# Two stream encoder layer: the first 256 tokens transposed on TensorE during the modulation, modulation weights loaded by rows, modulation columns applied as scalars

## The chip, the core and the metric

One core of a Trainium2 chip. The metric is device time in microseconds, the median of several executions. One further execution was taken with the hardware profiler; all rows below are from it.

## What is computed

One layer for a prompt of 2048 tokens and a sample of 64 tokens with a cache of 128, model width 1024. The reference, cut to what matters here:

```python
mod = jax.nn.silu(c) @ w_ada + b_ada                 # (1024) @ (1024, 3072)
shift, scale, gate = jnp.split(mod, 3, axis=-1)
h = rms_norm(x, norm_g) * (1.0 + scale[:, None, :]) + shift[:, None, :]
u = h @ w_in                                         # columns: qa, ka, va, za, qb, kb, vb, fb, zb
...
oa_blk = diff_attention(...)                         # 4 heads, two score maps each
ob_blk = forgetting_attention(...)                   # 8 heads, score bias from cumulated log forget values
...
o = jnp.concatenate([ga, gb], axis=-1) @ w_out       # ga, gb: outputs times silu(z)
return x + gate[:, None, :] * o
```

So nothing of the projection can start before shift and scale are known, and they need the first 2048 columns of w_ada (8 MB).

## The kernel before, in words

**Order of the work.** Every instruction is first recorded in a plan, with a position; the class Plan then gives each a due time from estimated durations, a latency table and the table SHIFT (one offset per kind of operation and stage), and writes for each engine (PE, ACT, DVE, POOL and the DMA queue SP) one fixed order. Engines work in their order and wait for each other by semaphores. So a change of one cost or offset moves instructions everywhere.

**Numbers.** Matrices are split into two fp16 parts, hi and lo, under scales that are powers of two; a product is three fp16 matmuls. The scale of h comes from a bound on its peak (`sig_h`), that of a weight group from its peak (`w_max`, `w_peak`, `w_sigma`), after which `w_split` makes hi on ACT and lo on DVE, slice by slice, in a ring of 17 buffers.

**Main part.** w_in is worked through in eight groups of 512 columns (order 0, 1, 4, 5, 6, 7, 2, 3); group 0 and 1 run interleaved. For each of 8 token blocks of 256: project (q, 24 matmuls of 512 columns per 128 tokens and group), evacuate to u, normalize, rotate (POOL), transpose u on PE (tr), scores S, exponentials (E), probabilities split and transposed by DMA (PB to PT), values (po), output og. The transposed h of all blocks (hT) is kept in DRAM for the later groups. At the end og is projected by w_out (y).

**The start, which the change touches.** SP issues in order: conditioning vectors, constants, group 0's eight weight slices (wc), then 8 modulation tiles (wada) with the first 256 tokens x_0 and x_1 between, then group 1's slices. Each wada tile holds two k-slices of one half of the columns (`load_ada`: 512 shift and 512 scale columns, so rows of 2 KB). `mod_mm` multiplies them by silu(c) of prompt and sample (2 weight columns) into two column groups of 32 PSUM partitions; first all eight k of half 0, then of half 1. After each half: `mod_evac` (ACT shift rows, DVE (1 + scale) * norm_g), `mod_max` (peaks), `mod_rows` (PE spreads the prompt's row over 128 partitions), `mod_store` (rows to DRAM, from where `mod_load` later spreads them over partitions for the other blocks). For the first 256 tokens `h_first` applies the rows with tokens on partitions (4 passes a half), then `h_first_split` makes hi and lo and `h_first_trans` transposes them by DMA into hT, which the first projection matmuls q of group 0 read.

Matmuls into po that have ident_b on both sides (`warm`) compute nothing; they only keep PE busy before and between these steps. Group 1's peak is spread over the partitions through DRAM (`spread`, `gather`: tiles wmx_d and wrow), group 0's by a transpose and a matmul (`all_max_mm`).

Of the kernel before, what the change touches and what calls it, by code (L numbers as in the profile page):

```python
# [41 lines left out]
class Plan:  # L42
# [24 lines left out]
        'ep_square ACT': (1222, 7059, 69075, 100316, 33946, 17761, -559, 7791, -55499),
        'ep_square DVE': (-19737, -11205, -6053, -6235, 13891, -12021, 5467, -9194, -18777),
        'ep_square SP d': (17731, 2644, -20421, 44685, -453, 17057, 7365, -5250, -5933),
        'ep_trans PE': (-8510, 1413, 20757, 14554, 4162, -22993, -38513, -7700, 0),  # L70
        'ep_v ACT': (77357, 78843, 94474, 106969, 15393, 26795, 14839, 59051, 0),
        'ep_v DVE': (123205, 212871, 14149, 83229, 170299, 16014, -443, 779, 0),
        'f_evac ACT': (0, 283107, 0, 0, 0, 0, 0, 0, 0),
        'f_evac DVE': (0, 28121, 0, 0, 0, 0, 0, 0, 0),
        'first h0 ACT': (-47637, 0, 0, 0, 0, 0, 0, 0, 0),
        'first h0 DVE': (39992, 0, 0, 0, 0, 0, 0, 0, 0),
        'first h0 SP d': (-43600, 0, 0, 0, 0, 0, 0, 0, 0),
        'first h1 ACT': (20737, 0, 0, 0, 0, 0, 0, 0, 0),
        'first h1 DVE': (-3029, 0, 0, 0, 0, 0, 0, 0, 0),
        'first h1 SP d': (-3083, 0, 0, 0, 0, 0, 0, 0, 0),  # L80
        'first w ACT': (-1750, 0, 0, 0, 0, 0, 0, 0, 0),
        'first w DVE': (2329, 0, 0, 0, 0, 0, 0, 0, 0),
        'first w PE': (-14065, 0, 0, 0, 0, 0, 0, 0, 0),
        'first w POOL': (14606, 0, 0, 0, 0, 0, 0, 0, 0),
        'first x ACT': (-27378, 0, 0, 0, 0, 0, 0, 0, 0),
        'first x POOL': (148021, 0, 0, 0, 0, 0, 0, 0, 0),
# [9 lines left out]
        'gate_out ACT': (0, 0, 2849, 0, 0, 0, 0, 0, 0),  # L96
        'gate_out SP d': (0, 0, 77357, 0, 0, 0, 0, 0, 0),
        'gate_scale DVE': (0, 0, 0, 0, 0, 0, 0, 942, 38016),
        'h_load SP d': (-15270, 27231, 30875, 38614, 21795, -15328, 60179, -34016, 0),
# [455 lines left out]
def hybrid_layer_kernel(ctx: ExitStack, tc: tile.TileContext, x_prompt, x_sample, cache_a_k, cache_a_v,  # L555
# [1371 lines left out]
```

## Time and profile before

| | |
|---|---|
| median of 3 runs | 1626.23 us (1624.32 to 1629.85) |
| the profiled execution, its own time | 1624.04 us |
| its span (first to last instruction) | 1622.3 us |
| busy: PE, DVE, ACT, POOL | 1441.1, 1261.6, 928.9, 495.6 us |
| mean granted clock of TensorE | 0.966 of full |
| DMA | 298.5 MB, mean 184 GB/s |
| first projection matmul | at 70.3 us of the span |

In the rows an instruction is named by engine, operation and its tiles (out<-in). Every operation is issued from one helper, so all have the line L551, and tiles tell them apart. A wait in brackets is the idle time of that engine before the row, with what ended it. PE is the matmul part of TensorE, SPq the DMA queue's issues. The clock of 1.00 is 2.4 GHz, 0.50 is 1.2 GHz.

### The profile page before, as it was taken

To read this page: it belongs to the slowest core of one execution; us is meant where nothing else is said; L and a number is where in the kernel's file an instruction comes from. 1 tells how busy PE (TensorE), PEld (TensorE's weight loads), DVE (VectorE), ACT (ScalarE), POOL (GpSimd) and SP (SyncE) were. 2 spreads that over 40 slices of the span, in tenths; PEclk is the share of its full clock that TensorE was granted. 3 is DMA by queue.
4 is the path that set the end of the run, shared out by engine and by line. 5 is a ranking of instruction groups with operands and counts; after the bars stand their busy time and mean duration, and the time that the engine had idled before them with its cause. 6 is when DMAs were issued, how large, how long until landed. Compare 5 with 4: busy or idle time off the path is not lost. (4 is left out here: it accounts for less than half of the span.)

```text
span 1622.3 us, 29643 instructions
## 1 busy us (share of the span) xinstructions
PE 1441.1 (89%) x10900; PEld 729.1 (45%) x10900; DVE 1261.6 (78%) x2619; ACT 928.9 (57%) x1768; POOL 495.6 (31%) x620
## 2 busy tenths in 40 slices
PE   7499987888999988998889889988999899698998
PEld 3144444443454444444444444444444454344443
DVE  4588999978969886988678867986899789797431
ACT  2257765655567665775667656865665566453100
POOL 0056663324322121111212112112355354412322
PEclk9699999989999999999999999999999999899999
DMA  9758789957978899999999999999858664889772
GB/s 314 127 156 195 198 186 233 157 110 178 208 152 175 199 201 208 199 212 209 217 164 210 196 197 215 206 192 203 204 151 153 132 156 124 159 168 231 199 196 70
DMA packets 630414, 298.50 MB, mean 184 GB/s; under 512 B 513183, under 2 KB 601007, under 8 KB 623484
## 3 DMA queue, kind: packets, MB, share of 16 engines
q1 hardware_dynamic: 630268, 296.61, 85.1%
q8 instruction: 85, 1.39, 0.4%
q14 instruction: 61, 0.49, 0.1%
HBM read 129.12 MB, written 43.16 MB: 106 GB/s over the span
## 5 line engine op out<-in xcount | busy, mean ns | idle before, releaser
L551 PE MATMUL q<-wc,hT 128*128 128x512 f16 x3072 | 733.4, 383 | 27.3 <-DMA hT<-hl 17.3
L551 PEld LDWEIGHTS <-hT 128*128 128x128 f16 x3328 | 293.8, 98 | 336.6 <-issue 31.8
L551 ACT ACTIVATE E<-E,st 128x128 f32<-128x128 f32 (+15 forms) x256 | 305.9, 1196 | 158.7 <-DVE st L551 80.6
L551 PE MATMUL po<-VT,PT 128*128 128x128 f16 x3808 | 247.7, 215 | 82.3 <-DMA PT<-PB 44.6
L551 PEld LDWEIGHTS <-PT 128*128 128x128 f16 x3808 | 213.3, 100 | 154.1 <-DMA PT<-PB 69.2
L551 PE MATMUL S<-KT,qT 64*128 64x512 f16 (+3 forms) x1920 | 227.2, 355 | 17.8 <-DVE E L551 14.8
L551 DVE SCALAR_TENSOR_TENSOR PB<-E,PB 128x128 f16<-128x128 f32 (+15 forms) x128 | 164.2, 1298 | 33.7 <-ACT PB L551 32.9
L551 PE MATMUL y<-wc,ogT 128*128 128x512 f16 (+1 forms) x800 | 177.1, 380 | 2.5 <-DVE os_e L551 1.3
L551 POOL TENSOR_SCALAR rs<-rs 128x8 f32<-128x8 f32 (+1 forms) x72 | 20.6, 285 | 518.4 <-DVE rs L551 491.9
L551 ACT ACTIVATE PB<-E 128x128 f16<-128x128 f32 (+15 forms) x128 | 138.3, 1102 | 46.3 <-DMA PT<-PB 45.7
L551 DVE CUSTOM_DVE_ANT_0 E<-S,nk,cf 128x1024 f32<-128x1024 f32 (+7 forms) x128 | 131.5, 1045 | 42.6 <-PE S L551 42.4
L551 PEld LDWEIGHTS <-qT 64*128 64x128 f16 x1920 | 83.9, 95 | 143.6 <-issue 77.4
L551 DVE TENSOR_SCALAR_CACHE_REDUCE E<-S,cf 128x1024 f32<-128x1024 f32 (+7 forms) x128 | 131.4, 1042 | 13.0 <-PE S L551 12.7
L551 POOL TENSOR_TENSOR u<-u,gain 128x512 f32<-128x512 f32 (+1 forms) x72 | 96.1, 1335 | 98.1 <-DVE u L551 23.7
L551 POOL TENSOR_TENSOR rs<-rs,mhalf 128x8 f32<-128x8 f32 (+1 forms) x72 | 118.3, 1643 | 6.0
L551 PEld LDWEIGHTS <-ogT 128*128 128x128 f16 (+1 forms) x800 | 75.8, 98 | 95.9 <-issue 10.9
L551 ACT ACTIVATE u<-q,us 128x384 f32<-128x384 f32 x128 | 73.1, 572 | 75.4 <-PE q L551 37.3
L551 ACT ACTIVATE PB<-E,st 128x128 f16<-128x128 f32 (+7 forms) x64 | 76.6, 1198 | 41.1 <-DVE E L551 14.3
L551 DVE SCALAR_TENSOR_TENSOR PB<-E,st,PB 128x128 f16<-128x128 f32 (+8 forms) x64 | 87.6, 1369 | 9.7 <-ACT PB L551 9.4
L551 POOL TENSOR_TENSOR yt<-yt,xr 128x512 f32<-128x512 f32 (+1 forms) x34 | 44.0, 1295 | 142.4 <-DVE yt L551 116.0
L551 POOL TENSOR_SCALAR oar<-oar 128x1 f32<-128x1 f32 (+1 forms) x68 | 38.2, 562 | 155.6 <-ACT og L551 152.7
L551 ACT ACTIVATE og<-po,us 128x128 f32<-128x128 f32 x128 | 45.9, 359 | 60.9 <-PE po L551 51.5
(210 smaller groups left out, 1778.8 us busy)
## 6 DMA issues: line engine op xcount, KB each, us to landing
hT<-hTd SPq DMA_DIRECT2D x53, 1024.0 KB
out_dram<-u SPq DMA_DIRECT2D x128, 128.0 KB
wc<-in_w_in_dram SPq DMA_DIRECT2D x32, 256.0 KB
wada<-in_w_ada_dram SPq DMA_DIRECT2D x16, 512.0 KB
x<-in_x_prompt_dram SPq DMA_DIRECT2D x16, 512.0 KB
hTd<-hT SPq DMA_DIRECT2D x16, 512.0 KB
ogd<-og SPq DMA_DIRECT2D x64, 128.0 KB
nk<-nck_d SPq DMA_DIRECT2D x16, 512.0 KB
```

Of the source, the lines that this page charges most:

```text
L551: fn(*a, **kw)
```

## The change

- wada tiles hold one k-slice of all 2048 columns (rows of 8 KB, for the last three tiles two rows of 4 KB). `mod_mm(k)` multiplies all four column groups (half and shift or scale) per k.
- One DVE pass evacuates all four groups (adding 0 or 1 by `mod1`, multiplying by 1 or norm_g in `grow`), one takes the peaks. PE transposes the rows, so that shift and scale stand as columns with the model dimension on partitions (`mcol`, already times `sig_h`).
- The first 256 tokens are multiplied by their root mean square on ACT (in `h_first_x`) and transposed by PE into PSUM while the modulation runs (x_0 after k = 4, x_1 after k = 6). `h_first(k)` then applies scale and shift as two per-partition scalars and makes hi and lo straight in hT: 8 x (DVE, ACT, DVE) on 128x256. The four DMA transposes are gone.
- The rows go to DRAM only after that. Group 1's peak goes through PE too.
- Fewer warming matmuls: 88 instead of 102.
- The planner's costs of a matmul with few weight columns and of early DMA are changed, and the whole table SHIFT.

```diff
     SHIFT = {
...
-        'mod DVE': (-41547, 0, 0, 0, 0, 0, 0, 0, 0),
...
-        'w_sigma DVE': (-87292, 37584, 108307, 13840, 127334, -17687, -9035, 0, 0),
...
+        'w_sigma DVE': (-62083, 179110, 2508, 16863, 28799, -16180, 137089, 0, 0),
+        'w_sigma PE': (-27708, 0, 0, 0, 0, 0, 0, 0, 0),
...
-            return max(25.0, n / 2.4 * (0.55 if self.count(ar[0]) <= 32 else 1) + 2.5)
+            return max(25.0, n / 2.4 * (0.16 if self.count(ar[0]) <= 32 else 1) + 2.5)
...
-            return (560.0 if eng == "SP" else 400.0), tot * size / 300.0 * max(1.0, 512.0 / max(row, 64))
+            return (560.0 if eng == "SP" else 400.0), tot * size / (390.0 if self.pos < -90 else 300.0) * max(1.0, 512.0 / max(row, 64))
...
+    def load_ada(k):
+
+        tag, bufs = ADA_TAGS[k]
         if tag == "PT":
-            t = [st([128, 2, 512], F32, f"wada{n}_{i}", tag=tag, bufs=bufs) for i in range(2)]
+            t = [st([128, D], F32, f"wada{k}_{i}", tag=tag, bufs=bufs) for i in range(2)]
+            for i in range(2):
+                sp.dma_start(out=t[i], in_=wada_v[:, k, i * D:i * D + D])
         else:
-            t = st([128, 2, 2, 512], F32, f"wada{n}", tag=tag, bufs=bufs)
+            t = st([128, 2, D], F32, f"wada{k}", tag=tag, bufs=bufs)
+            sp.dma_start(out=t.rearrange("p s c -> p (s c)"), in_=wada_v[:, k, 0:2 * D])
             t = [t[:, i] for i in range(2)]
...
+    dve.memset(grow, 1.0)
...
-        if g:
+        if g > 1:
             spread(g, m)
...
-        if g == 0:
-            all_max_mm(mod_ps["S0"][:, 512:1024], m[:, 0:1], m[:, 1:2])
+        if g < 2:
+            all_max_mm(O_tile() if g else mod_ps["S0"][:, 512:1024], m[:, 0:1], m[:, 1:2])
...
-    WARM0, WARM1 = 9, 10
+    WARM0, WARM1 = 4, 3
...
+    def mod_mm(k):
+        for hf in range(2):
+            for s in range(2):
+                c, o = 32 * (2 * hf + s), s * D + hf * 512
+                if k == 0:
+                    pe.matmul(mod_ps["p"][c:c + 2, :], ones[0:1, 0:2], bada[0:1, o:o + 512], start=True, stop=False)
+        for hf in range(2):
+            for s in range(2):
+                c = 32 * (2 * hf + s)
+                pe.matmul(mod_ps["p"][c:c + 2, :], cs[:, k, :], ada_w[k][s][:, hf * 512:hf * 512 + 512], start=False, stop=(k == KC - 1))
+
+    def mod_evac():
+
+        dve.scalar_tensor_tensor(out=modr, in0=mod_ps["p"], scalar=mod1, in1=grow, op0=ALU.add, op1=ALU.mult)
+        dve.tensor_reduce(out=hb[:, 0:1], in_=modr, axis=AX, op=ALU.max, apply_absolute_value=True)
+
+    def mod_cols():
+
+        c = mod_ps["c"] = Q_tile("modc")
+        for q in range(4):
+            pe.transpose(c[:, q * 128:q * 128 + 128], modr[:, q * 128:q * 128 + 128], ident)
...
+    def h_first_x(t):
+
+        x = x_t[0, t]
+        act.activation(out=x, in_=x, func=AF.Copy, scale=hrs[0, t][:, 1:2])
+        for k in range(KC):
+            c = k % 4 * 256 + t * 128
+            pe.transpose(mod_ps[f"S{k // 4}"][:, c:c + 128], x[:, k * 128:k * 128 + 128], ident)
+
+    def h_first(k):
+
+        if k == 0:
             hT[0, 0] = st([128, 16, 256], F16, "hT0_0", tag="hT", bufs=2)
...
+        p = mod_ps[f"S{k // 4}"][:, k % 4 * 256:k % 4 * 256 + 256]
+        x = x_t[0, k // 4][:, k % 4 * 256:k % 4 * 256 + 256]
+        hi, lo = hT[0, 0][:, 2 * k, :], hT[0, 0][:, 2 * k + 1, :]
+        dve.tensor_scalar(out=x, in0=p, scalar1=mcol[:, 1, k:k + 1], scalar2=mcol[:, 0, k:k + 1], op0=ALU.mult, op1=ALU.add)
+        act.activation(out=hi, in_=x, func=AF.Copy)
+        dve.tensor_tensor(out=lo, in0=x, in1=hi, op=ALU.subtract)
...
+    for k in range(KC):
+        plan.event(-96 + 2 * k)
+        mod_mm(k)
+        plan.event(-95 + 2 * k)
+        warm(WARM0)
+        if k in (4, 6):
+            plan.event(-95 + 2 * k + 0.5, name="first x")
+            h_first_x((k - 4) // 2)
+    plan.event(-80.5, True, "mod")
+    mod_evac()
+    mod_cols()
...
+    plan.event(-79.9, True, "mod")
+    pe.transpose(hp[0:1, 0:128], hb[:, 0:1], ident)
+    dve.tensor_reduce(out=hb[0:1, 2:3], in_=hp[0:1, 0:128], axis=AX, op=ALU.max)
...
+    pe.matmul(hp[:, 128:129], hmix, hb[0:1, 2:3], start=True, stop=True)
+    dve.tensor_scalar(out=hb[:, 4:5], in0=hp[:, 128:129], scalar1=2.0 ** -46, scalar2=None, op0=ALU.max)
+    sig_h = sigma(hb[:, 4:5], "sig_h", floor=False)
+    dve.tensor_scalar(out=mcol.rearrange("p s (h q) -> p s h q", h=2),
+                      in0=mod_ps["c"].rearrange("p (q h s r) -> p s h q r", q=4, h=2, s=2)[:, :, :, :, 0],
+                      scalar1=sig_h[:, 0:1], scalar2=None, op0=ALU.mult)
...
+    for k in range(KC):
+        plan.event(-79.5 + 0.1 * k, True, "first h")
+        h_first(k)
+    plan.event(-70, name="second x")
+    mod_store()
```

What this does to the order. First PE at the modulation; modp collects the modulation, wada are its weights, mod_ are PSUM tiles of the start, x the first tokens. Before, from the last k of half 0 on (102 warming matmuls, 12 of them between the k of half 0, stand ahead of this):

```order
L551 MATMUL modp<-wada_144,cs 2x512 x2
L551 MATMUL modp<-wada_145,cs 2x512 x4
L551 MATMUL modp<-wada_146,cs 2x512 x4
L551 MATMUL mod_141<-modr,ident 128x512
L551 MATMUL mod_140<-modr,ident 128x512
L551 MATMUL modp<-bada,ones 2x512
L551 MATMUL modp<-wada_148,cs 2x512
L551 MATMUL modp<-bada,ones 2x512
```

After, from k = 3 to k = 5 (88 warming matmuls and k = 0 to 2 stand ahead):

```order
L547 MATMUL modp<-wada_148,cs 2x512 x4
L547 MATMUL modp<-wada_150,cs 2x512 x4
L547 MATMUL mod_142<-ident,x_0_149 128x128 x4
L547 MATMUL mod_143<-ident,x_0_149 128x128 x4
L547 MATMUL modp<-wada_0_151,cs 2x512
L547 MATMUL modp<-wada_1_152,cs 2x512
L547 MATMUL modp<-wada_0_151,cs 2x512
L547 MATMUL modp<-wada_1_152,cs 2x512
```

One run per half, with the spreading of half 0's rows between the two, has become one run over k. In it stand the transposes of x_0, and behind k = 6 those of x_1; all warming matmuls stand ahead of it.

Then DVE from the modulation's evacuation to h of the first tokens (wmx: peaks of group 1's weight slices). Before:

```order
L551 SCALAR_TENSOR_TENSOR modr<-modp,grow 2x512
L551 TENSOR_REDUCE wmx_199<-wc_114 128x1
L551 TENSOR_REDUCE wmx_199<-wc_115 128x1
L551 TENSOR_REDUCE wmx_199<-wc_116 128x1
L551 TENSOR_REDUCE hb<-modr 2x1
L551 TENSOR_REDUCE wmx_199<-wc_117 128x1
L551 TENSOR_REDUCE wmx_199<-wc_118 128x1
L551 TENSOR_REDUCE wmx_199<-wc_119 128x1
L551 TENSOR_REDUCE hb<-modr 2x1
L551 TENSOR_REDUCE wmx_199<-wc_120 128x1
```

After:

```order
L547 SCALAR_TENSOR_TENSOR modr<-modp,mod_137,grow 128x512
L547 TENSOR_REDUCE hb<-modr 128x1
L547 TENSOR_REDUCE wmx_199<-wc_130 128x1
L547 TENSOR_REDUCE hb<-modh 1x1
L547 TENSOR_REDUCE wmx_199<-wc_114 128x1
L547 TENSOR_SCALAR hb<-modh 128x1
L547 TENSOR_SCALAR sig_h_e<-hb 128x1
L547 TENSOR_SCALAR sig_h<-sig_h_e 128x1 x2
L547 TENSOR_SCALAR mcol<-modc,sig_h 128x16
L547 TENSOR_SCALAR x_0_149<-mod_142,mcol 128x256 x2
L547 TENSOR_TENSOR hT_0_172<-x_0_149,hT_0_172 128x256 x2
```

Two weight maxima instead of six stand in the chain from modr to sig_h.

Last, DVE at the peak of group 1 (wm_1) in the changed kernel; us_203 is the scale for its splits, the first of which follows a few rows later:

```order
L547 TENSOR_REDUCE wm_1_200<-wmx_199 128x1
L547 TENSOR_SCALAR us_162<-ws_161,sig_h 128x1
L547 SCALAR_TENSOR_TENSOR x_173<-x_173,hr_0_175,gsP 128x1024
L547 TENSOR_REDUCE wm_1_200<-po 1x1
L547 TENSOR_TENSOR x_173<-x_173,shP 128x1024
L547 COPY wm_1_200<-po 128x1
L547 TENSOR_SCALAR ws_e<-wm_1_200 128x1
L547 TENSOR_SCALAR ws_e<-ws_e 128x1
L547 TENSOR_SCALAR ws_202<-ws_e 128x1
L547 COPY us_203<-ws_202 128x1
L547 TENSOR_SCALAR ws_202<-ws_e 128x1
```

Before, these steps read wrow, which had come through DRAM, and the first split came right behind:

```order
L551 TENSOR_REDUCE wm_1_200<-wrow_201 128x1
L551 TENSOR_SCALAR ws_e<-wm_1_200 128x1
L551 TENSOR_SCALAR ws_e<-ws_e 128x1
L551 TENSOR_SCALAR ws_203<-ws_e 128x1
L551 COPY us_204<-ws_203 128x1
L551 TENSOR_SCALAR ws_203<-ws_e 128x1
L551 TENSOR_SCALAR us_204<-ws_203,sig_h 128x1
L551 TENSOR_SCALAR us_204<-us_204 128x1
L551 TENSOR_SCALAR us_204<-ws_203,sig_h 128x1
L551 SCALAR_TENSOR_TENSOR wc_121<-wc_130,us_204,wc_121 128x512
```

The maximum now comes by PE and stands between two passes over x.

## Rows read from the trace of the kernel before

**Rows 1.** The page, section 1 (busy time, share of the span, instructions) and section 2 (tenths busy in 40 slices of 40.6 us).
```profile
PE 1441.1 (89%) x10900; PEld 729.1 (45%) x10900; DVE 1261.6 (78%) x2619; ACT 928.9 (57%) x1768; POOL 495.6 (31%) x620
...
PE   7499987888999988998889889988999899698998
...
PEclk9699999989999999999999999999999999899999
DMA  9758789957978899999999999999858664889772
```
**Rows 2.** The waits of PE from 70 us to the end: who waited for whom, us in total, times, the longest.
```profile
PE po L551 <- DMA PT<-PB: 44.6, 32, 6.1
PE po L551 <- DVE og L551: 18.8, 20, 3.3
PE q L551 <- DMA hT<-hl: 17.3, 3, 14.5
```
**Rows 3.** PE's timeline of the modulation: start us, us from the first start to the last end, what, xcount (an fp32 matmul is two passes, so x20 are ten).
```profile
19.23 1.02 PE L551 MATMUL modp<-wada,cs 128*2 128x512 f32 x2
...
25.84 4.46 PE L551 MATMUL modp<-wada,cs 128*2 128x512 f32 x20
33.16 1.13 PE L551 MATMUL mod<-modr,ident 2*128 2x512 f32 x4 [2.86 <-DVE modr L551]
...
35.16 1.72 PE L551 MATMUL modp<-wada,cs 128*2 128x512 f32 x2
...
38.60 8.79 PE L551 MATMUL modp<-wada,cs 128*2 128x512 f32 x30
```
**Rows 4.** Stretches of two us: length, busy time of PE, PEld, DVE, ACT, POOL (instructions), granted clock, DMA share, GB/s.
```profile
34.00:36.00 2.00, 2.00 (x6) 0.17 (x4) 1.86 (x3) 0.90 (x2) 0.74 (x2) 0.84 1.05 387
36.00:38.00 2.00, 2.00 (x4) 0.08 (x2) 1.43 (x3) 0.00 (x0) 0.00 (x0) 0.50 1.06 368
...
42.00:44.00 2.00, 2.00 (x12) 0.45 (x10) 0.00 (x0) 0.00 (x0) 0.00 (x0) 0.96 0.90 149
```
**Rows 5.** The same columns for the first 32 and the first 38 us.
```profile
0.00:32.00 32.00, 24.85 (x141) 13.04 (x141) 12.50 (x37) 7.30 (x12) 1.25 (x12) 1.00 0.93 304
...
0.00:38.00 38.00, 29.69 (x151) 13.59 (x151) 17.70 (x44) 9.34 (x15) 2.74 (x16) 0.97 0.95 316
```
**Rows 6.** The timeline of the start: ScalarE's weight passes of group 0 (8), the square of x_0, POOL's power for it, the square of x_1.
```profile
26.17 5.06 ACT L551 ACTIVATE wc<-wc,us 128x520 f16<-128x520 f32 x8 [21.47 <-DVE ws L551]
...
31.75 1.04 ACT L551 ACTIVATE junk<-x 128x1024 f32<-128x1024 f32 x1
...
33.25 0.55 POOL L551 TENSOR_TENSOR hr<-hr,mhalf 128x1 f32<-128x1 f32 x1
33.74 1.06 ACT L551 ACTIVATE junk<-x 128x1024 f32<-128x1024 f32 x1 [0.86 <-DMA x<-in_x_prompt_dram]
```
**Rows 7.** The timeline from the end of the modulation to the first projection matmuls and the first weight passes of group 1.
```profile
47.42 0.59 ACT L551 ACTIVATE modr<-modp 2x512 f32<-2x512 f32 x1 [12.53 <-PE modp L551]
48.04 0.70 DVE L551 SCALAR_TENSOR_TENSOR modr<-modp,grow 2x512 f32<-2x512 f32 x1 [7.57 <-ACT modr L551]
...
53.27 0.68 DVE L551 TENSOR_REDUCE hb<-modr 2x1 f32<-2x512 f32 x1
...
54.90 0.28 DVE L551 TENSOR_REDUCE hb<-mod 2x1 f32<-2x128 f32 x1
...
56.23 0.22 DVE L551 TENSOR_SCALAR sig_h<-sig_h_e 128x1 int32<-128x1 int32 x2
...
63.42 5.73 SPq L551 DMA_TRANSPOSE hT<-hl  x2
...
70.31 1.03 PE L551 MATMUL q<-wc,hT 128*128 128x512 f16 x2 [14.49 <-DMA hT<-hl]
70.33 0.72 ACT L551 ACTIVATE wc<-wc,us 128x512 f16<-128x512 f32 x1 [2.00 <-DVE us L551]
...
71.08 0.75 DVE L551 SCALAR_TENSOR_TENSOR wc<-wc,us,wc 128x512 f16<-128x512 f32 x1 [0.17 <-ACT wc L551]
```
**Rows 8.** PE's timeline behind it: the first matmuls of group 1, the first transposes of u, the first matmuls of token block 1.
```profile
81.33 2.35 PE L551 MATMUL q<-wc,hT 128*128 128x512 f16 x9
...
95.78 0.66 PE L551 MATMUL tr<-ident,u 128*128 128x128 f32 x4 [0.68 <-POOL u L551]
96.35 0.59 PE L551 MATMUL q<-wc,hT 128*128 128x512 f16 x2
```
**Rows 9.** The timeline of all engines from 80 us: a 128x1024 pass that makes h, one that splits it, the rotation input u of block 0.
```profile
81.56 1.28 DVE L551 SCALAR_TENSOR_TENSOR x<-x,hr,gsP 128x1024 f32<-128x1024 f32 x1
...
86.41 1.28 DVE L551 SCALAR_TENSOR_TENSOR hl<-x,sig_h,hl 128x1024 f16<-128x1024 f32 x1
...
92.03 0.68 DVE L551 TENSOR_TENSOR u<-u,rs 128x512 f32<-128x512 f32 x1
```
**Rows 10.** The transposed u (tile tr): durations in ns, minimum, median, maximum, then first and last start.
```profile
L551 PE MATMUL tr<-ident,u x256: 270/273/474, 95.8 to 1392.8; 128*128 128x128 f32 x128
...
L551 ACT ACTIVATE qT<-tr x64: 359/375/400, 96.8 to 1393.1; 128x256 f16<-128x256 f32 x64
...
L551 DVE TENSOR_TENSOR qT<-tr,qT x64: 402/416/426, 97.7 to 1395.7; 128x256 f16<-128x256 f32 x64
```
**Rows 11.** A stretch of 50 us, columns as in group 4.
```profile
170.00:220.00 50.00, 46.99 (x368) 23.32 (x367) 47.83 (x83) 35.72 (x75) 30.62 (x41) 1.00 0.75 184
```

More of the change, by code (lines that the diff above doesn't have):

```diff
@@ L67 @@
[L67 to L86, printed above, removed]
[9 rows of a table removed]
[L96 to L99, printed above, removed]
@@ new lines @@
+        'first h DVE': (-7095, 0, 0, 0, 0, 0, 0, 0, 0),
+        'first w ACT': (-54367, 0, 0, 0, 0, 0, 0, 0, 0),
+        'first w DVE': (74742, 0, 0, 0, 0, 0, 0, 0, 0),
+        'first w PE': (66499, 0, 0, 0, 0, 0, 0, 0, 0),
+        'first w POOL': (35838, 0, 0, 0, 0, 0, 0, 0, 0),
+        'first x ACT': (29080, 0, 0, 0, 0, 0, 0, 0, 0),
+        'first x PE': (6006, 0, 0, 0, 0, 0, 0, 0, 0),
+        'first x POOL': (-10905, 0, 0, 0, 0, 0, 0, 0, 0),
[9 rows of a table added]
+        'gate_out ACT': (0, 0, 32507, 0, 0, 0, 0, 0, 0),
@@ new lines @@
+        'second x ACT': (78919, 0, 0, 0, 0, 0, 0, 0, 0),
+        'second x POOL': (-48541, 0, 0, 0, 0, 0, 0, 0, 0),
+        'second x SP d': (-17432, 0, 0, 0, 0, 0, 0, 0, 0),
+        'small ACT': (30811, 0, 0, 0, 0, 0, 0, 0, 0),
+        'small DVE': (-927, 0, 0, 0, 0, 0, 0, 0, 0),
+        'small POOL': (84973, 0, 0, 0, 0, 0, 0, 0, 0),
+        'small SP d': (68836, 0, 0, 0, 0, 0, 0, 0, 0),
+        'smp_P ACT': (0, -85002, -141622, -85920, -70232, 51281, -86043, -85916, -101814),
+        'smp_P PE': (0, -16207, -19657, -16258, -25469, -25864, -25384, -16207, -27759),
@@ L853, in hybrid_layer_kernel @@
     hb = st([128, 8], F32, "hb")
-    dve.memset(hb, 2.0 ** -46)
-    def mod_mm(hf, k):
-        for s in range(2):
-            c, o = 32 * (2 * hf + s), s * D + hf * 512
-            if k == 0:
-                pe.matmul(mod_ps["p"][c:c + 2, :], ones[0:1, 0:2], bada[0:1, o:o + 512], start=True, stop=False)
-            pe.matmul(mod_ps["p"][c:c + 2, :], cs[:, k, :], ada_w[4 * hf + k // 2][k % 2][:, s, :], start=False, stop=(k == KC - 1))
-    def mod_evac(hf):
-        a, b = slice(64 * hf, 64 * hf + 2), slice(64 * hf + 32, 64 * hf + 34)
-        p = mod_ps["p"]
-        act.activation(out=modr[a, :], in_=p[a, :], func=AF.Copy)
-        dve.scalar_tensor_tensor(out=modr[b, :], in0=p[b, :], scalar=1.0, in1=grow[b, :], op0=ALU.add, op1=ALU.mult)
@@ L869, in mod_max @@
-    def mod_max(hf):
-        for s in range(2):
-            a = slice(64 * hf + 32 * s, 64 * hf + 32 * s + 2)
-            dve.tensor_reduce(out=hb[a, s:s + 1], in_=modr[a, :], axis=AX, op=ALU.max, apply_absolute_value=True)
-    def mod_rows(hf):
-        for s in (1, 0):
-            c = 64 * hf + 32 * s
-            p = mod_ps[hf, s] = mod_ps[f"S{s}"][:, 0:512] if hf == 0 else Q_tile(f"mod{2 + s}")
-            plan.event(plan.pos + 0.1, name="mod")
-            pe.matmul(p, ident[c:c + 2, c:c + 1].broadcast_to([2, 128]), modr[c:c + 2, :], start=True, stop=True)
@@ new lines, in mod_evac, with mod_store @@
+    def mod_evac():
[5 more added lines that the diff above has]
+            pe.transpose(c[:, q * 128:q * 128 + 128], modr[:, q * 128:q * 128 + 128], ident)
+    def mod_store():
+        for hf in range(2):
+            for s in range(2):
+                c = 64 * hf + 32 * s
+                sp.dma_start(out=mod_d[:, s, hf * 512:hf * 512 + 512], in_=modr[c:c + 2, :])
@@ L1050, in hybrid_layer_kernel @@
             h_stat(j, t)
-    plan.event(-70, name="mod")
-    hmix = st([2, 128], F32, "hmix", tag="rt", bufs=1)
-    dve.memset(hmix, 33.0)
-    dve.memset(hmix[0:1, :], 1.0)
-    hp = mod_ps["S1"][:, 512:1024]
-    pe.transpose(hp[0:2, 0:128], hb[:, 0:2], ident)
-    dve.tensor_reduce(out=hb[0:2, 2:3], in_=hp[0:2, 0:128], axis=AX, op=ALU.max)
-    pe.matmul(hp[:, 128:129], hmix, hb[0:2, 2:3], start=True, stop=True)
-    dve.tensor_copy(hb[:, 4:5], hp[:, 128:129])
-    sig_h = sigma(hb[:, 4:5], "sig_h", floor=False)
-    for t in range(2):
-        plan.event(-70, name=f"first h{t}")
-        for hf in range(2):
-            h_first(t, hf)
-        for hf in range(2):
-            h_first_split(t, hf)
-            h_first_trans(t, hf)
     plan.event(-50, name="small")
```

247 lines of the change are left out of this document (111 added, 136 removed), and 31 rows, old and new, of the table SHIFT.

## The prediction

> **What bounds the kernel now.** I read the page first. PE is busy for 1441 of 1622 us, but its second slice of 40 us stands at 4 tenths, and there TensorE's clock is granted at 0.6; elsewhere PE stands at 7 to 9 tenths [rows 1]. So there are two losses: the start, and some 150 us of small waits behind it. The chain of waits is led there by the transposed probabilities (44.6 us in 32 waits), then by output tiles (18.8 us), and 14.5 us of the 17.3 us on hT is one wait, the first projection matmul at 70.3 us [rows 2]. After it PE hardly waits for a long stretch, and its last slices are full again with output matmuls [rows 1], so what PE gains early reaches the end unless a later wait takes it back.
>
> In the timeline of the start the reader is to see four steps. The modulation's first half ends at 30.3 us; PE is idle until 33.16; then the clock is 0.84, then 0.50, and the second half takes until 47.4 us although its weights are there [rows 3, 4]. Behind it come 22.9 us without projection work: evacuation at 47.42 and 48.04, the peak of the rows only at 53.27 (weight maxima stand between), the scale at about 56.4, the DMA transposes issued at 63.42, the first matmul at 70.31 [rows 7].
>
> **Arrival of the modulation weights.** The loads ahead of them and their bytes stay the same, only in rows of 8 or 4 KB. Through x_1 they are 9.69 MB. By 32 us 304 GB/s x 32 = 9.73 MB had moved [rows 5], and ScalarE, waiting, began on x_1 at 33.74 [rows 6]: 1.8 us from byte to use. From 32 to 38 us it is (316 x 38 - 304 x 32) / 6 = 380 GB/s. So pairs k4, k5, k6, k7 (1.05 MB each; 8.12, 9.17, 10.74, 11.79 MB in all) are usable at 29.6, 32.3, 36.5 and 39.2 us. I take no gain from the longer rows: the DMA engines are already full there.
>
> **The modulation on PE.** Ten matmuls in alternating column groups take 4.46 us, 0.45 each; one whose two passes stand alone takes 1.02 with its tail [rows 3]. Four groups instead of two: I keep 0.45, on the assumption that a matmul's two passes enter in order and the second waits for the first, however many groups there are. So a k costs 1.8 us. The Trainium skill, TensorEngine Tiling (Array Packing), section Theoretical Speedup, gives up to 4x for a dimension of 32 or less; by it a k would cost about 1 us and the end of the modulation move 0.8 us earlier. The two groups of this trace give 1.02 / 0.45 = 2.3x.
>
> k4 then runs 29.6 to 31.4. The x_0 transposes stand next in PE's queue, and everything behind them waits for ScalarE: its eight weight passes end at 31.23, the row statistic takes 33.80 - 31.75 = 2.05, and the new scaling pass of 128x1024 is taken like the square of as many elements, 1.06 [rows 6]: 34.4. Eight fp32 transposes, four of which take 0.66 [rows 8]: 1.3, to 35.7.
>
> Here the clock decides. Before, an idle stretch of 2.9 us was followed by half clock 2.2 us after work resumed, and full clock came back 7.9 us after it [rows 3, 4]. The new idle stretch, 31.4 to 34.4, is as long, and all 88 warming matmuls stand ahead of the modulation now, none in it. With the fall at 36.6 and the return at 42.3: k5 ends at 38.4, k6 at 41.9, the x_1 transposes (ready at 37.6) at 43.4, k7 at 45.3. Without a fall: 42.5. I take 45.3 and keep 42.5 as the other end. The Trainium skill, TensorE: Matmul & The Clock Gate, Part 1, says that idleness halves the array's clock and activity releases it; this trace agrees (0.50 at 36 to 38 us), and the rule speaks against moving the warming work.
>
> **From the modulation to the first projection.** New chain: evacuation 0.70, peak 0.68, one weight maximum of the same width, 0.68, that stands ahead, the 128-wide maximum 0.28 [rows 7], another weight maximum 0.68 (it covers PE's small matmul), the scale with its four short operations 0.6 (two take 0.22 in [rows 7]), the columns 0.2, two 128x256 passes from PSUM where the first releases ScalarE (nearest 0.416; I take 0.42), ScalarE's copy 0.375 [rows 10], and some 0.3 of semaphore gaps: 4.9 us, between 4.5 and 5.5. First matmul at 50.2 instead of 70.31: PE leads by 20.1 us. The four DMA transposes, the two mod broadcasts on PE and the VectorE passes that stood between 53 and 61 us are gone with that; the 16 new passes (6.7 us) feed PE as it goes.
>
> **What is late next.** The second group's weights. Their peak no longer goes through DRAM but through PE, in the order behind 36 of q0's matmuls. Before, 36 matmuls took 70.31 to 81.33 [rows 7, 8], the first six us at half clock, as now: the transpose is reached at 61.2. VectorE by then: 16 passes to 56.1, five maxima 3.4, a scalar 0.35, one g 0.28, the last maximum 0.68 and short ones 0.3: 61.2 as well. Then, in the order, 1.28 for x [rows 9], 0.28 row maximum, as much as the first for x again, copy 0.16, four short ones 0.76: ScalarE's first weight pass of group 1 at 65.0, where before it was at 70.33 [rows 7, 9]. So a lead of 20 is already 5.3 there, and PE, with q0 done at about 66, is fed by this chain. From VectorE's first such pass to the rotation input u it was 71.08 to 92.03, 20.95 us [rows 7, 9]; the new order leaves two x passes and one hl pass (1.28 each [rows 9], 3.8) for later: 17.2, so 82.9. From there to the first matmul of the next token block was 96.35 - 92.03 = 4.3 [rows 8, 9]: 87.2, a lead of 9.1 us. The eighth weight slice, now queued on SP behind the modulation's four stores and two x loads, should land some 7 us before its maximum (issued near 49, behind 1.05 MB); without that cover it would cost one for one.
>
> **The rest of the order** is replanned by a new table. Counted in the order, PE has on average slightly more matmul columns between a row's scores and its first use of the transposed row than before, and in some rows fewer. I take nothing, plus or minus 8 us.
>
> **Sum**: the profiled run's own 1624.0 less 9.1 is 1614.9; it lies 2.2 us under the median of the three runs. I predict 1615. About 0.3% (4.9 us) is what a measurement can tell from no change.
>
> **Rivals.**
> 1. The lead stays whole. If the clock holds and the peak of group 1 is through PE by 59, its weights start 5 us earlier, and what VectorE has left over is absorbed in its thinner stretches. Then up to 20 us stay: 1604. For it: PE is busy for 47 of 50 us from 170 to 220 [rows 11]. Against it: the order puts three long VectorE passes around that peak.
> 2. VectorE is the limit. It is busy for 47.8 of 50 us from 170 to 220 [rows 11], and its own lead is 5.3 us at group 1's weights; the 3.8 us of passes it left behind come back. Then at most 5 us stay, 1619 to 1624, which is mostly no measurable change. Against it: PE is as full there, at 47.0.
> 3. Slower. DMA is at 9 tenths and more in about half the slices [rows 1], and PE's longest bill is the transposed rows [rows 2]. If the new order issues those transposes later, each of the 32 waits grows; with 0.65 us each it is 21 us, less 9: 1636. It decides from (9.1 + 4.9) / 32 = 0.44 us a wait.
>
> **Chances.** Forecast (a lead of 4.9 to 16 us, 1608 to 1619 by itself) 0.47; rival 1 0.22; rival 2 0.19; rival 3 0.12. Faster: 0.45 + 0.22 + 0.05 = 0.72; same 0.16; slower 0.12. The range 1598 to 1628 reaches to rival 1 with 6 us from a better order, and takes in rival 2; it leaves out most of rival 3 and a better order still.
>
> **What would show it.** Clock near 0.5 in part of 36 to 42 us and the last modulation matmul near 45 (42.5: the clock held). First projection matmul near 50 (over 55: the peak chain is mis-sized). First weight pass of group 1 near 65, PE waiting for these passes before 85, first matmul of block 1 near 87. Waits on transposed rows near 45 us in total. The prediction is wrong if this last sum moves by more than 14 us, or if the lead at 87 is above 14 or below 5.

## The result, and the profile after

The changed kernel takes 1585.03 us (median of 4 runs, 1579.52 to 1585.88), the kernel before beside it 1626.46 (1624.32 to 1629.85): a ratio of 0.9736, 95% interval 0.9708 to 0.9764, so 41 us faster. Run again on another chip it came to 0.974 (0.9713 to 0.9768). I had predicted 1615 us, 1598 to 1628: right in sign, wrong in size. The profiled execution took 1584.51 us, with a span of 1582.7.

The page of the changed kernel, sections 1 and 2 (a slice is 39.6 us now), against [rows 1]:

```profile
PE 1430.8 (90%) x10901; PEld 726.2 (46%) x10901; DVE 1263.9 (80%) x2624; ACT 932.3 (59%) x1772; POOL 500.3 (32%) x620
...
PE   7799999889999998989889899988998999799998
...
PEclk8899999989999999999999999999999999899999
DMA  9768889749997999999999999999567656689862
```

PE is busy 10.3 us less than before (1430.8 for 1441.1): 8.2 of it up to the first matmul of token block 1 (58.3 for 66.4), 2.1 behind it. The second slice has gone from 4 to 7 tenths, the clock of the first two stands at 0.8, and the 6 and the 7 further back have become one 7.

PE's timeline of the modulation, which answers to [rows 3] (x8 is one k, four matmuls of two passes):

```profile
17.97 1.04 PE L547 MATMUL modp<-wada,cs 128*2 128x512 f32 x8
...
21.65 1.04 PE L547 MATMUL modp<-wada,cs 128*2 128x512 f32 x8 [1.18 <-DMA wada<-in_w_ada_dram]
...
24.14 1.89 PE L547 MATMUL modp<-wada,cs 128*2 128x512 f32 x8 [1.14 <-DMA wada<-in_w_ada_dram]
26.63 1.89 PE L547 MATMUL modp<-wada,cs 128*2 128x512 f32 x8 [0.60 <-DMA wada<-in_w_ada_dram]
30.39 1.89 PE L547 MATMUL modp<-wada,cs 128*2 128x512 f32 x8 [1.88 <-DMA wada<-in_w_ada_dram]
32.28 1.97 PE L547 MATMUL mod<-ident,x 128*128 128x128 f32 x8
34.18 3.65 PE L547 MATMUL modp<-wada,cs 128*2 128x512 f32 x16
37.76 1.10 PE L547 MATMUL mod<-ident,x 128*128 128x128 f32 x8
38.79 1.61 PE L547 MATMUL modp<-wada,cs 128*2 128x512 f32 x8
```

and of the weight loads (PEld puts a matmul's weights into TensorE) the one for the second half of k = 7:

```profile
39.36 0.10 PEld L547 LDWEIGHTS modp<-wada,cs 128*2 128x2 f32 x6 [0.49 <-DMA wada<-in_w_ada_dram]
```

Stretches of it, with the columns of [rows 4]:

```profile
24.00:30.00 6.00, 3.77 (x16) 0.21 (x16) 5.22 (x9) 5.97 (x10) 0.00 (x0) 0.50 1.01 416
...
34.00:36.00 2.00, 2.00 (x11) 0.31 (x10) 0.00 (x0) 1.15 (x2) 0.46 (x2) 0.50 1.02 406
36.00:38.00 2.00, 2.00 (x14) 0.35 (x9) 0.00 (x0) 1.15 (x1) 0.28 (x1) 0.84 1.05 369
...
46.00:48.00 2.00, 2.00 (x10) 0.85 (x9) 1.94 (x6) 0.83 (x2) 0.00 (x0) 0.50 0.94 309
```

The reader is to see three things. PE waits for the weights (DMA wada) ahead of k = 1 to 4, and its weight loads wait for them once more within k = 7, until 39.36. A k takes 1.04 us at full clock and 1.89 at half, and half clock came as early as the stretch from 24 us. The end at 40.4 us so follows k7's arrival. Behind it the timelines of VectorE, PE and ScalarE, to the first projection matmul and the first weight pass of group 1, against [rows 7]:

```profile
40.45 0.75 DVE L547 SCALAR_TENSOR_TENSOR modr<-modp,mod,grow 128x512 f32<-128x512 f32 x1 [10.21 <-PE modp L547]
...
44.12 0.99 DVE L547 TENSOR_SCALAR x<-mod,mcol 128x256 f32<-128x256 f32 x2
```
```profile
45.16 1.03 PE L547 MATMUL q<-wc,hT 128*128 128x512 f16 x2 [2.03 <-ACT hT L547]
...
55.97 0.27 PE L547 MATMUL po<-ident,wm 128*1 128x128 f32 x1
...
61.74 0.39 PE L547 MATMUL q<-wc,hT 128*128 128x512 f16 x1 [1.05 <-ACT wc L547]
...
80.81 0.98 PE L547 MATMUL tr<-ident,u 128*128 128x128 f32 x4 [4.00 <-POOL u L547]
81.58 0.63 PE L547 MATMUL q<-wc,hT 128*128 128x512 f16 x1
```
```profile
24.03 5.07 ACT L547 ACTIVATE wc<-wc,us 128x520 f16<-128x520 f32 x8 [19.38 <-DVE ws L547]
...
31.08 1.15 ACT L547 ACTIVATE x<-x,hr 128x1024 f32<-128x1024 f32 x1 [0.95 <-POOL hr L547]
...
60.97 0.71 ACT L547 ACTIVATE wc<-wc,us 128x512 f16<-128x512 f32 x1
```

So PE's projection starts 25.2 us earlier than at 70.31, group 1's weights 9.4 us earlier than at 70.33, and token block 1 14.8 us earlier than at 96.35 [rows 7, 8]. The start itself varies: three further traces with the same order up to there, on other chips, have the first matmul of block 1 at 78.26, 79.52 and 79.92 us, so its lead is 15 to 18 us. At the end the lead is 39.6 us of span: some 25 us were gained after 82 us. Nearly all of that is PE's waiting. From the first matmul of block 1 to the end it waited 143.3 us before and waits 120.4 now (all rows of that view added). The part for VectorE fell from 71.8 to 43.1 us, the part for transfers went from 47.4 to 50.5, those for ScalarE and POOL moved by about 3 us or less. The longest rows of the changed kernel, from 81.5 us, beside [rows 2]:

```profile
PE po L547 <- DMA PT<-PB: 50.5, 39, 5.4
PE po L547 <- DVE og L547: 15.7, 22, 2.8
...
PE S L547 <- DVE E L547: 11.3, 12, 6.5
...
PE q L547 <- DVE g L547: 1.6, 1, 1.6
```

and of the kernel before, from 96.3 us (the last row is one of several single waits that are gone):

```profile
PE S L551 <- DVE E L551: 14.8, 14, 7.5
...
PE q L551 <- DVE g L551: 6.6, 1, 6.6
```

### The profile page after: what moved, and what is told of

It is laid out like the page before. It is cut to its first block, busy times and chain, and to the rows that moved or that the text cites. A ratio compares the mean times of both kernels' runs of the same rounds, so it can differ in the third digit from the quotient of the medians.

```text
span 1582.7 us, 29638 instructions
## 1 busy us (share of the span) xinstructions
PE 1430.8 (90%) x10901; PEld 726.2 (46%) x10901; DVE 1263.9 (80%) x2624; ACT 932.3 (59%) x1772; POOL 500.3 (32%) x620
## 5 line engine op out<-in xcount | busy, mean ns | idle before, releaser
L547 PE MATMUL q<-wc,hT 128*128 128x512 f16 x3072 | 743.2, 385 | 10.5 <-DVE g L547 2.7
L547 PE MATMUL po<-VT,PT 128*128 128x128 f16 x3808 | 247.2, 215 | 76.1 <-DMA PT<-PB 50.5
L547 PE MATMUL S<-KT,qT 64*128 64x512 f16 (+3 forms) x1920 | 223.2, 351 | 15.6 <-DVE E L547 11.3
L547 POOL TENSOR_SCALAR rs<-rs 128x8 f32<-128x8 f32 (+1 forms) x72 | 26.0, 361 | 509.9 <-DVE rs L547 495.1
L547 POOL TENSOR_TENSOR u<-u,gain 128x512 f32<-128x512 f32 (+1 forms) x72 | 101.4, 1408 | 91.8 <-DVE u L547 19.4
L547 POOL TENSOR_SCALAR oar<-oar 128x1 f32<-128x1 f32 (+1 forms) x68 | 31.8, 467 | 204.0 <-ACT og L547 201.4
L547 DVE SCALAR_TENSOR_TENSOR PB<-E,st,PB 128x128 f16<-128x128 f32 (+7 forms) x64 | 89.4, 1398 | 3.1 <-ACT PB L547 3.1
```

What stands on the lines that cost most here:

```text
L547: fn(*a, **kw)
```

## Experiments

Chips differ: the kernel before takes 1626 us on one and 1637 on another. So verdicts go by the ratio to the kernel before on the same chip, and 0.001 is 1.6 us.

**Start and order taken apart.** The engines' order is written out once and given to the program, so that the first part of one kernel's order can be followed by the rest of the other's. Only this is changed, with the list ISSUE_ORDER that it reads:

```diff
     plan.schedule()
+    plan.order = [plan.ops[i] for i in ISSUE_ORDER]
     plan.issue()
```

> The changed kernel; only the order of the engines is altered, and nothing is left out: up to the first projection matmul of token block 1 (81.6 us) it is that of the changed kernel, from there to the end the order of the kernel before. Theory A (the re-planned rest is itself worth the 22 us by which the lead grows from 17.5 us at 80 us to 39.6 us at the end): about 1585 + 22 = 1607 us, 1603 to 1611. Theory B (the old order would have done as well; the early start frees the engines, and the later waits never arise): 1585 to 1590 us.

Measured: 0.9888 (0.9855 to 0.9922), 18 us faster than before and 25 slower than the changed kernel.

> The kernel before up to its first matmul of token block 1 (96.35 us), from there the order of the changed kernel. Nothing is left out. Theory A: the 22 us come without the new start, 1626 - 22 = 1604 us, 1600 to 1608. Theory B: no gain without the early start, 1622 to 1628 us.

Measured: 0.9901 (0.9867 to 0.9936), 16 us faster than before, where Theory A had 22.

The 17.5 us in the first expectation was read from PE's remaining busy time, in which lost records count; by the first matmul of block 1 it is 14.8. Theory A holds in the main: the rest of the order is worth 16 us behind the old start, and 25 behind the new one (each within some 6 us, so that the two do not surely differ). Theory B falls: with the old rest the start's lead stays what it is and grows no further. To see this along the run, take the moments at which VectorE evacuates KT (64 times in each trace), the n-th in each, and subtract it from that of the kernel before:

```
n-th KT          0      4      9     15     40     60
before, at    97.3  150.9  258.3  410.1  951.5 1344.6
lead of
changed       14.7   11.5   28.5   31.0   39.7   38.3
new start,
old rest      16.7   17.9   17.5   19.9   14.7   10.5
old start,
new rest      -2.3   -7.3    8.8   14.0   13.1   12.3
```

The splices ran on a chip on which the kernel before is some 4 to 6 us slower than in this trace, so their late leads are understated by about that. In both kernels with the new rest the lead grows by 16 to 17 us from the 4th to the 9th (14 and 11 from the 0th, as it first falls), whichever start they have.

> The changed kernel with the old order only in a stretch: from the first matmul of token block 1 to the first one of projection slot 12 (about 82 to 243 us), before and behind it the new order. Nothing is left out. In this stretch the lead grew from 17.5 to 28.6 us. Theory A: 1585 + 11 = 1596 us, 1592 to 1600. Theory B: 1585 to 1588 us. If it is above 1604 us, the seams of the two orders cost by themselves, and the splices tell less.

Measured: 0.9842 (0.9805 to 0.988), 17 us slower than the changed kernel, where 11 were expected: with an error of some 7 us this bears out Theory A and tells no difference from 11.

> The kernel before with the new order only from the first matmul of token block 1 to the first one of projection slot 12 (about 96 to 272 us). Nothing is left out. Theory A: 1626 - 11 = 1615 us, 1611 to 1619, and the wait of 6.6 us at 255.8 us, where PE waits for VectorE's g, is gone. Theory B: 1622 to 1628 us.

Measured: 0.998 (0.9956 to 1.0004), no change that can be told, where Theory A had 11 us; the time is in Theory B's range. So the parts of the order are not independent. Taking the middle out costs about the lead that arose there, and putting it in alone keeps almost nothing: the lead of 8.8 us at the 9th KT is 1.1 at the 35th. Whether a seam of two orders costs something by itself was not tried.

**Single places.** In the kernel before, three passes that PE waits long for are moved within VectorE's order. The first of them:

```diff
 L551 TENSOR_SCALAR E_7_0_500,st_7_0_501<-S_7_0_0_498,cf_194 128x1024
+L551 SCALAR_TENSOR_TENSOR g_0_6_481<-g_0_6_481,q_6_1_482 128x128
 L551 TENSOR_REDUCE rs_6_503<-sq_6_502 128x8
...
 L551 TENSOR_TENSOR u_6_480<-u_6_480,rs_6_503 128x2x256
-L551 SCALAR_TENSOR_TENSOR g_0_6_481<-g_0_6_481,q_6_1_482 128x128
```

> The kernel before with three places of VectorE's order altered, nothing else and nothing left out: the g that PE waits 6.58 us for at 255.8 us goes ahead of a row's score maximum and two probability passes, the VT pass that PE's 3.76 us at 1093.0 us hang on goes ahead of two score passes, and the maximum of the second output weights' row, for which VectorE itself idles 5.58 us at 1408.6 us, goes behind the two score passes that PE waits 7.54 us for. Theory C (the order's gain sits in single places where VectorE does something else first): each of the three waits falls to about 1 us, in all 13 us: 1626 - 13 = 1613 us, 1610 to 1618. Theory D (such a wait only moves to the next row, since VectorE and the DMA transposes are as full as PE): 1622 to 1630 us, with new waits within 50 us behind each place.

Measured: 0.9987 (0.9971 to 1.0002). Theory D. PE's timeline of the kernel before at the three places, and then of this one (taken on another chip):

```profile
255.76 1.01 PE L551 MATMUL q<-wc,hT 128*128 128x512 f16 x2 [6.58 <-DVE g L551]
```
```profile
1092.99 0.91 PE L551 MATMUL po<-VT,PT 128*128 128x128 f16 x14 [3.76 <-DVE wmx L551]
```
```profile
1409.63 0.58 PE L551 MATMUL S<-KT,qT 64*128 64x512 f16 x1 [7.54 <-DVE E L551]
```
```profile
250.66 0.61 PE L551 MATMUL q<-wc,hT 128*128 128x512 f16 x2 [1.06 <-DMA hT<-hl]
...
257.17 2.74 PE L551 MATMUL S<-KT,qT 64*128 64x512 f16 x12 [4.94 <-ACT qT L551]
```
```profile
1105.52 1.30 PE L551 MATMUL po<-VT,PT 128*128 128x128 f16 x14 [4.03 <-DMA PT<-PB]
```
```profile
1412.64 0.82 PE L551 MATMUL S<-KT,qT 64*128 64x512 f16 x5 [1.67 <-DVE E L551]
...
1423.95 3.70 PE L551 MATMUL po<-VT,PT 128*128 128x128 f16 x33 [5.21 <-DMA PT<-PB]
```

The 6.58 us fell to 1.06, and 4.94 came back at once, on the evacuation of qT. The 3.76 us for VectorE became 4.03 for PT. The 7.54 became 1.67, and 5.21 for PT followed. Over the whole trace behind block 1's first matmul, PE's waits on VectorE fell from 71.8 to 52.9 us and those on transfers rose from 47.4 to 63.3; all of them together are 144.9 us, against 143.3.

> The changed kernel with three places of VectorE's order altered, nothing left out: u of the second group ahead of a pass over x (PE waits 4.00 us for it at 80.8 us), four short passes on the sample's sE ahead of a probability pass (4.47 us at 324.4 us), and the maximum of the second output weights' row behind two score passes (6.55 us at 1370.6 us). Theory C: 3 + 2.5 + 5.5 = 11 us, 1585 - 11 = 1574 us, 1570 to 1579. Theory D: 1582 to 1588 us.

Measured: 0.9753 (0.9733 to 0.9773), within the error the same as the changed kernel. Two of the moves did not do what the expectation says: VectorE's pass on u came 4.1 us earlier (71.36 for 75.44), but POOL's next one only 0.8, which is no more than the whole stretch came early there, behind a pass of its own that waited for ScalarE, and PE waits 5.43 us for u instead of 4.00; and sE's passes came ahead of some short ones and a weight pass only, not of the probability pass (3.17 instead of 4.47). At 1370 us 6.55 became 0.92, and 4.81 for PT followed. A single wait was not worth its length in any of these places; that this is because VectorE and the transposes are as full as PE is argued from the waits that came in its stead, and not shown by itself.

**Is the gain in the table or in the plan?** The planner's old estimates are put back into the changed kernel:

```diff
-            return max(25.0, n / 2.4 * (0.16 if self.count(ar[0]) <= 32 else 1) + 2.5)
+            return max(25.0, n / 2.4 * (0.55 if self.count(ar[0]) <= 32 else 1) + 2.5)
...
-            return (560.0 if eng == "SP" else 400.0), tot * size / (390.0 if self.pos < -90 else 300.0) * max(1.0, 512.0 / max(row, 64))
+            return (560.0 if eng == "SP" else 400.0), tot * size / 300.0 * max(1.0, 512.0 / max(row, 64))
```

> The changed kernel with the planner's two old estimates (0.55 for narrow matmuls, 300 GB/s for early DMA) and the new table; nothing left out. Both estimates concern the start alone, yet PE's order differs in thousands of rows. Theory E (the table fits one plan only; any other plan made with it loses the order's gain): 1600 to 1612 us. Theory F (the table's offsets are good for any such plan): 1583 to 1590 us.

Measured: 0.9958 (0.9934 to 0.9982), 35 us slower than the changed kernel: even more than Theory E allowed. Then one constant that says nothing of the chip, on the same chip as the changed kernel once more:

```diff
-    OVERLAP = dict(PE=0.0, ACT=97.0, DVE=78.0, POOL=40.0)
+    OVERLAP = dict(PE=0.0, ACT=99.0, DVE=78.0, POOL=40.0)
```

> The changed kernel once more, beside the three that follow. Both theories: 0.974 of the kernel before, 0.971 to 0.977.

> The changed kernel with one constant of the planner altered, the overlap of two ScalarE instructions from 97 to 99 ns, which says nothing new of the chip; the engines' orders come out otherwise in thousands of rows. Nothing is left out. Theory E (start and work are the same, but the order's gain belongs to the one plan that the table was made for): 15 to 40 us slower than the changed kernel, 0.983 to 0.998 of the kernel before. Theory F (the table is good in general): within 5 us of it, 0.971 to 0.978.

> The kernel before with the same constant altered from 97 to 99 ns. Nothing is left out. Theory E (each table fits its own plan): 15 to 40 us slower than the kernel before, 1.009 to 1.025 of it. Theory G (the old table was a loose one, and what the new order gains is that it is fitted at all): within 5 us of the kernel before, 0.997 to 1.003.

Measured: 0.974 (0.9713 to 0.9768), 0.9862 (0.9833 to 0.9891), 1.0063 (1.0039 to 1.0087). And another constant:

```diff
-    PE_CLOCK = 1.07
+    PE_CLOCK = 1.08
```

> The changed kernel with another constant of the planner altered, the factor on PE's estimated durations from 1.07 to 1.08; a third plan from the new table. Nothing is left out. Theory E (the order's gain belongs to the one plan): 0.983 to 1.000 of the kernel before, like the two plans already run (0.986 and 0.996). Theory F (those two were unlucky): 0.970 to 0.980.

Measured: 0.9974 (0.9952 to 0.9996). The start is as early as in the changed kernel in all three altered plans (block 1's first KT leads by 14.9 to 16.7 us), and at the 60th KT the leads are 5.0, 2.5 and -9.3 us (the changed kernel on the second chip: 23.9; these chips are some 10 us slower than that of the trace of before). So three plans made with the new table are 20 to 38 us slower than the one it came with: Theory E. An altered plan with the old table is 10 us slower than its own, which lies between the ranges of Theory E and Theory G and decides for neither. As far as four altered plans can tell, the gain belongs to one plan. PE's waits say the same: behind block 1's first matmul they come to 120 to 137 us in the seven traces with the new rest, and to 143 to 156 in the nine with the old rest or an altered plan (one trace of either kind has the other order in its middle).

In the first of them (the overlap of 99 ns) PE's waits from 80 us, to be held against those of the changed kernel above:

```profile
PE po L547 <- DVE og L547: 19.6, 25, 3.6
...
PE q L547 <- ACT u L547: 10.3, 1, 10.3
```

It waits once for 10.3 us on ScalarE, which the changed kernel does nowhere; in the plan with the old estimates such a wait is 9.9 us.

**Group 1's peak.** In the changed kernel it goes through DRAM again:

```diff
-        if g > 1:
+        if g:
             spread(g, m)
...
-        if g < 2:
-            all_max_mm(O_tile() if g else mod_ps["S0"][:, 512:1024], m[:, 0:1], m[:, 1:2])
+        if g == 0:
+            all_max_mm(mod_ps["S0"][:, 512:1024], m[:, 0:1], m[:, 1:2])
```

> The changed kernel, its order kept, with group 1's peak spread through DRAM again as in the kernel before (a store and a load on the queue SP in place of a transpose and a matmul on PE). Nothing is left out. Before, the load alone took 6.2 us from issue to VectorE (63.01 to 69.25). If the first weight pass of group 1 (now at 60.97 us) waits for it, it comes at about 67 and all of this reaches the end: 1585 + 6 = 1591 us, 1588 to 1594. If a wait of PE behind it (4.00 us for u at 80.8 us) is from elsewhere and takes it up: 1584 to 1587 us.

Measured: 0.9837 (0.9821 to 0.9853), 16 us slower than the changed kernel, where 6 were expected; both of the ranges named fall short. The queue SP, VectorE, PE and ScalarE in its trace:

```profile
55.98 0.33 SPq L547 DMA_DIRECT2D wmx_d<-wm  x1
63.86 0.33 SPq L547 DMA_DIRECT2D wrow<-wmx_d  x1
```
```profile
68.53 0.29 DVE L547 TENSOR_REDUCE wm<-wrow 128x1 f32<-128x128 f32 x1 [8.83 <-DMA wrow<-wmx_d]
```
```profile
70.38 0.61 PE L547 MATMUL q<-wc,hT 128*128 128x512 f16 x1 [11.82 <-ACT wc L547]
```
```profile
69.61 0.72 ACT L547 ACTIVATE wc<-wc,us 128x512 f16<-128x512 f32 x1 [8.72 <-DMA small<-in_lam_q_dram]
```

The store stands at 55.98 and the load that needs it at 63.86, 7.9 us later; 4.7 us after that VectorE has the row. Weights start 8.6 us later than at 60.97 (the bracket on ScalarE's row names another load; the scale that these weights need came behind VectorE's row of 68.53), and PE waits 11.82 us. The other 7 us are lost further on. The reverse, the same edit forwards in the kernel before:

> The kernel before, its order kept, with group 1's peak spread by a transpose and a matmul on PE in place of the store and load through DRAM, right behind the last pass that makes h of the first tokens. Nothing is left out. The first weight pass of group 1 would come near 62.5 us in place of 70.33. Theory H (the new start and the peak on PE need each other: here PE begins its projection at 70.3 us anyway and hardly waits for these weights): 0 to 2 us gained, 0.998 to 1.001. Theory I (the peak is worth its 8 us by itself): 0.993 to 0.996.

Measured: 0.9934 (0.9906 to 0.9961), 11 us faster: Theory I, and my reason for H was wrong. First SP in the kernel before, then SP and PE here:

```profile
54.89 0.35 SPq L551 DMA_DIRECT2D wmx_d<-wm  x1
...
63.01 0.32 SPq L551 DMA_DIRECT2D wrow<-wmx_d  x1
```
```profile
59.15 2.73 SPq L551 DMA_TRANSPOSE hT<-hl  x2
```
```profile
62.49 1.04 PE L551 MATMUL q<-wc,hT 128*128 128x512 f16 x2
```

In the kernel before, the load of the peak stood on SP for its store, 8.1 us, and the transposes of the first h stood behind it until 63.42 [rows 7]. Without it they go at 59.15, and the projection begins at 62.49 instead of 70.31. So 7.8 of the 14.5 us on hT in [rows 2] were not the chain of h at all, but two tiny transfers ahead of it in the queue. The 11 us (within some 4) stand beside 18 for the whole new start: as far as two runs on two chips can be compared, the peak alone gives more than half of that, and the other parts of the start, for which the kernel is named, add some 7 us, within some 7. The Trainium skill, DMA: Bandwidth & Descriptors, section Anatomy of one DMA — SWDGE (gpsimd) path, puts most of a transfer's fixed time, some 2 us, into the confirmation of the write, and says that this can be long where DRAM is written. That is told of transfers issued by GpSimd; here SP issued them, the order of events agrees, and 7.9 us among running loads is four times its figure.

**The clock.** 24 of the 88 warming matmuls are moved into PE's gaps between 40.4 and 45.2 us.

> The changed kernel, its order kept but for 24 of the 88 warming matmuls: 6 behind the last modulation matmul, 6 behind the peak's transpose, 12 behind the peak's matmul, in front of the first projection matmul, so that PE is busy between 40.4 and 45.2 us, where it now mostly waits. Nothing is left out. If that keeps the granted clock at 1.00, the first 24 projection matmuls, which now take until 50.1 us at 0.50, end 2.5 us earlier. Theory K (behind them PE waits for group 1's weights, whose first pass at 61.0 us hangs on VectorE): 0 to 0.5 us of that reach the first matmul of token block 1 and the end, 0.973 to 0.975 of the kernel before. Theory L (PE decides): 2 to 2.5 us, 0.972 to 0.973. The clock may fall all the same; then nothing changes.

Measured: 0.9753 (0.9714 to 0.9792), no change that can be told. Windows of it and the timelines of PE and ScalarE:

```profile
44.00:46.00 2.00, 1.41 (x13) 1.02 (x13) 1.79 (x9) 0.47 (x2) 0.00 (x0) 1.00 0.97 140
46.00:48.00 2.00, 1.76 (x11) 0.74 (x12) 1.94 (x5) 1.02 (x3) 0.00 (x0) 1.00 1.01 315
```
```profile
45.97 0.61 PE L547 MATMUL q<-wc,hT 128*128 128x512 f16 x2 [0.59 <-ACT hT L547]
...
47.79 0.61 PE L547 MATMUL q<-wc,hT 128*128 128x512 f16 x2 [0.24 <-ACT hT L547]
...
80.48 0.59 PE L547 MATMUL q<-wc,hT 128*128 128x512 f16 x2
```
```profile
60.13 0.70 ACT L547 ACTIVATE wc<-wc,us 128x512 f16<-128x512 f32 x1
```

The clock stayed at 1.00 through 48, and PE then waited for hT instead (0.59, 0.24), which VectorE and ScalarE make at their own pace. Group 1's weights come at 60.13, 0.8 us earlier, and block 1 at 80.48, 1.1 us earlier than at 81.58. That is between Theory K and Theory L and within the spread of the unaltered start (78.26 to 81.58), and the measured time cannot tell their 2 us apart: it stays open which of them holds.

## Why the prediction was wrong

**The step that failed is the rest of the order**, in its words "I take nothing, plus or minus 8 us". It is worth 16 us behind the old start and 25 behind the new one, where 8 was the bound. The count of matmul columns between a row's scores and its transposed probabilities could not tell this: waits on PT indeed stayed near 45 us (50.5), while those on VectorE fell by 29. The bound was wrong too. Altering a constant of the planner by 1 or 2% made the time 10 to 38 us longer, so the term had to carry some 20 us or more; that every line of the table had changed stood in the diff. That the order stood on the fast side of that spread could not be read from the trace of before.

**The start** was forecast at a lead of 9.1 us at block 1 and gave 14.8, just above the 14 that the prediction names as its own sign of being wrong; alone it makes 0.9888, 1608 us, inside the range. By its terms:
- *Arrival*: k7 usable at 39.2; its first matmul ran at 38.79, and the weights of its second half were there at 39.36. Right.
- *Pitch of a k*, taken as 1.8: 1.04 at full clock, 1.89 at half. The assumption that a matmul's second pass waits for its first, however many groups there are, fell: one matmul alone took 1.02 [rows 3], four in four groups take 1.04, 3.9 times as fast. The rule of the Trainium skill that I had set against it (TensorEngine Tiling (Array Packing), Theoretical Speedup: up to 4x) is borne out. Its price was not the 0.8 us of the prediction, though: in the prediction's own chain without a fall, a k of 1.04 lets k7 run from its arrival at 39.2 to 40.2, 2.3 us ahead of 42.5. In the trace it ends 1.04 us after its second half's arrival.
- *Clock*, taken to fall at 36.6 and put the modulation's end at 45.3: it fell by 24 us, where loads set the pace, stood at 0.50 through 36, and was back for k7. (The return was misread too: 0.96 from 42 to 44 in [rows 4] puts it at 42.16, 9.0 us after work resumed at 33.16 and not 7.9; the price of the fall would have been, by the same chain, about half a us higher.) The idle stretch of 3 us for x_0 did not come: ScalarE's weight passes began at 24.03 instead of 26.17, so scaling ended at 32.2, not 34.4. End 40.40, below even the 42.5 without a fall.
- *From there to the projection*: 4.9 us, measured 45.16 - 40.40 = 4.76. Right, and so the 5.0 us by which the projection came early (45.16 for 50.2) all arose ahead of 40.40: by the prediction's own numbers 2.8 are the fall that it feared (45.3 for 42.5) and 2.1 the pitch and the earlier x_0.
- *Group 1's weights*: 65.0, measured 60.97, the start's 5.0 us less one. PE reaches the peak's transpose at 55.97, which had been put at 61.2.
- *Block 1*: 87.2, measured 81.58. PE does wait for VectorE and POOL there (4.00 us for u), as said.

**The reading of before** had one fault that the experiments found: the wait on hT was put down to the chain of maxima, scale and passes, and the transposes' issue at 63.42 was taken as its end. That SP held them behind a load that waited for its own store was in the trace, in the row above.

**The rivals.** Rival 1, the lead stays whole, held behind block 1 only: 25.2 us at the projection were 14.8 there, but from then on the lead stayed, 16.7 and 19.9 us at the 0th and 15th KT behind the old rest. Its 1604 was near the 1608 measured for the start alone, though the clock, which it wanted to hold, did not. Rival 2 fell, since VectorE did not hold the lead back. Rival 3 fell: PT's waits grew by 6 us, not 21, and stayed within the 14 us that the prediction allows them. The case that came, rival 1 with a better order on top, stood in the text as one that the range leaves out.

## What to carry to other kernels

A planner's new table is not priced by reading its order, nor is it a better table: alter a constant that means nothing, time the plans, and take their spread (here 10 to 38 us) as the bound of any change that re-plans. A wait is not worth its length until a run says so: three waits of 4 to 8 us each, taken away, gave 2 us in all, within the error of nothing. And where a transfer is late, look at what stands ahead of it in its queue before pricing the chain that makes its data.

## What was not expected of the hardware

A store of 128 numbers and the load that reads them back took 12.6 us among running transfers (55.98 to 68.53), 7.9 of it until the load could be issued. Four fp32 matmuls of 2 columns in four column groups ran in 1.04 us, as long as one. Half clock from 24 to 36 us cost nothing at the modulation's end, as PE's weight load still waited for the last transfer at 39.36. The same program on two chips, the changed kernel's profiled executions: 1584.5 and 1602.8 us, with 50.5 and 58.5 us of PE's waits on the transposed probabilities (that execution is the slowest of the second chip's four, whose median is 1595.3); why the second chip's transposes are later stays open. Open as well is why the plan that came with the table fits so much better than its neighbours: the runs show that it does, and that it is not in the single places tried.
